# Two layers with experts and an attention block: two more weight slots, and GpSimd's small transfers on the ScalarE and SyncE queues

## The chip, the cores and the metric

The kernel runs on one core of a Trainium2 chip. The metric is the device time of one execution in microseconds. Of the kernel before there are three timed runs, 1488.46, 1492.85 and 1492.9 us, with a median of 1492.85 us, and one profiled execution of its own.

## The reference, cut to what matters

The input is 256 tokens of 1024 float32 values. A first block has two layers, each a mixer with a residual and layer norm, then a mixture of 16 experts with the same. A second block is one layer of attention and a gated feed-forward part with a short convolution.

```python
def ec_moe(x, w_router, w_gate, w_up, w_down):         # 16 experts, 32 tokens each
    aff = softmax(x @ w_router)
    gates, idx = lax.top_k(swapaxes(aff, 1, 2), 32)
    xin = x[bidx, idx]
    h = silu(xin @ w_gate[e]) * (xin @ w_up[e])         # 32x1024 @ 1024x1024, twice
    out = (h @ w_down[e]) * gates
    return zeros_like(x).at[bidx, idx].add(out)

x = layer_norm(ALPHA * x + mlstm_mixer(x), ln_g[0, 0], ln_b[0, 0])
x = layer_norm(ALPHA * x + ec_moe(x, layer 0), ln_g[0, 1], ln_b[0, 1])
x = layer_norm(ALPHA * x + gla_mixer(x), ln_g[1, 0], ln_b[1, 0])
x = layer_norm(ALPHA * x + ec_moe(x, layer 1), ln_g[1, 1], ln_b[1, 1])
h = x + moba_attention(rms_norm(x, attn_norm) @ w_qkv, rel_bias) @ w_o
h = h + conv_ffn(rms_norm(h, ffn_norm), w_up, conv_w, conv_b, w_down)
return rms_norm(h, final_norm)
```

## The kernel before, in words

**Stages.** In the profiled execution the first mixer (mLSTM) runs from 0 to some 140 us, the first layer's experts to 575, the second mixer (GLA) to 720, the second layer's experts to 1160, then the query, key and value products, attention and the output product to 1285, and the feed-forward part to the end.

**Weights.** All weights come as units of 1 MB, a tile of 128 partitions by 2048 float32 values, from the pool `big`, in one fixed order (`stream`). They are loaded by SyncE (SP) alone, at L141 where a unit is flat and at L147 where it is laid out by column blocks. An expert takes twelve units: four of `moe_w_gate`, four of `moe_w_up`, four of `moe_w_down`. A layer's experts therefore take 192 units. We number the units from the first gate unit of layer 0, so that layer 1's experts are units 208 to 399; expert e of a layer has its gate units at 12e to 12e+3, then up, then down.

**Slots.** `SLOTS` is the number of such tiles that may be in use. Working tiles of the mixers (`slab`) come out of the same pool, and `pump` loads on while there is room:

```python
    def pump():
        while stream and mem["wts"] < SLOTS - max(mem["keep"], mem["act"]):
            emit_load()
```

`keep` holds slots back for working tiles that will be wanted soon; it is 1 to 10 in the stages and rises at the end of a layer's experts (8 + 2i from expert 10, 14 + 2i from expert 14, where i is the layer).

**One expert.** TensorE multiplies the 32 picked tokens with the gate and up units (L978), ScalarE (ACT) applies the silu to the gate's product (L993), VectorE multiplies by the up product (L994), TensorE transposes (L998), VectorE copies (L1002), TensorE multiplies with the four down units (L1025), and ACT and VectorE copy the result out (L1037). The last expert of a layer has sums woven in (L987), warm-up products (L186), and its own down product (L1058, L1071). `extra` hangs other work on experts: `gla_prep` (L1170 to L1180) on expert 9 of layer 0, rows for the second mixer (`spread`, L342) on expert 12 of it, the tables of the relative bias (L1222) on experts 6 to 13 of layer 1 and their rows (`bucket_rows`, L1212 and L1213) on expert 5, and `attn_rows` (L342, L1235) on expert 14.

**What sets the order.** A scheduler orders the instructions of each engine when the kernel is built; each engine then runs its own list in order, and a step that waits holds all behind it on that engine. The transfers that SP and ACT issue share eight completion semaphores, DMAHW0 to DMAHW7, given out in turn over both engines. A transfer on one of them carries a wait for the transfer that had the semaphore before it. In the kernel before, where ACT issues only three transfers, all at the start, that means that SP keeps at most eight units on the way. The transfers that GpSimd (POOL) issues have semaphores of their own (DMASW). There are 26 of them: the rows of the layer norms (L342, L943), ten of `gla_prep` (L1170, L1175, and eight at L1180), two of `bucket_rows`, `attn_norm` (L1235), three of the convolution (L1287 to L1289), and the rows of the last norms (L342).

Of the kernel before, what the change touches and what calls it, by code (L numbers as in the profile page):

```python
# [10 lines left out]
F32 = mybir.dt.float32  # L11
# [6 lines left out]
P = 128  # L18
S = 256
# [7 lines left out]
RSQ = 1.5 ** (1 / 7)  # L27
RSQ_BITS = float(round(0x5F3759DF + 0.5 * math.log2(0.5 * RSQ) * (1 << 23)) - (1 << 31))

SLOTS = 25  # L30
NSPLIT = 3
NE0 = 1
E0 = 32 * NE0
# [11 lines left out]
def two_layer_mixer_moe_then_attention_kernel(  # L45
# [9 lines left out]
    nc = tc.nc  # L55

    const = ctx.enter_context(tc.tile_pool(name="const", bufs=1))
    big = ctx.enter_context(tc.tile_pool(name="big", bufs=SLOTS))
    work = ctx.enter_context(tc.tile_pool(name="work", bufs=3))
# [7 lines left out]
    def slab(dt=F32):  # L67
        mem["act"] += 1
        assert mem["act"] + mem["wts"] <= SLOTS, mem
        t = big.tile([P, 2048], dt, tag="slot", name="slab")  # L70
        return t
# [10 lines left out]
    def kcols(w, c0, n):  # L82
        return w[:, c0:c0 + n].rearrange("(k p) f -> p k f", p=P)
# [52 lines left out]
    def emit_load(parts=1):  # L136
        src = stream.pop()
        mem["wts"] += 1
        t = big.tile([P, 2048], F32, tag="slot", name="unit")
        if len(src.shape) == 2:  # L140
            nc.sync.dma_start(t[:, :2048], src)  # L141
            ready.insert(0, t[:, :2048].rearrange("p (k f) -> p k f", k=2))
            return
        v = t[:, :2048].rearrange("p (k f) -> p k f", k=src.shape[1])
        n = src.shape[2] // parts
        for j in range(parts):
            nc.sync.dma_start(v[:, :, j * n:j * n + n], src[:, :, j * n:j * n + n])  # L147
        ready.insert(0, v)
# [5 lines that stand above are left out]
    def take():  # L154
        if not ready:
            assert mem["act"] + mem["wts"] < SLOTS, mem
            emit_load()
# [14 lines left out]
    def aux():  # L172
        b = psp.tile([P, 512], F32, tag="aux", name="aux")
        return b
# [39 lines left out]
    x_tok = tok(xt)  # L214
    for t in range(2):
        nc.sync.dma_start(x_tok[:, t, :], x[0, t * P:(t + 1) * P, :])
    ones = const.tile([P, P], F32, name="ones")
    ones_row = ones[:, 0:1].to_broadcast([P, S])
    ident = const.tile([P, P], F32, name="ident")
    nc.gpsimd.memset(ones, 1.0)  # L220
    nc.gpsimd.affine_select(ident, ones, pattern=[[1, P]], compare_op=OP.is_equal, fill=0.0, base=0,
                            channel_multiplier=-1)
    gpad = slab()
# [41 lines left out]
    def open_split(n=NSPLIT, claim=False):  # L265
        wsp[:0] = [slab(F32R) for _ in range(n)]
        if claim:
            for t in wsp[:n]:
                nc.gpsimd.memset(t[:, 0:1].bitcast(F32), 0.0)
# [66 lines left out]
        tr[:] = [transposed(src, use, bank)]  # L336
        return h, l

    def spread(dst, tmp, *rows):
        n = 1024 * len(rows)  # L340
        for j, row in enumerate(rows):
            nc.gpsimd.dma_start(tmp[0:1, 1024 * j:1024 * j + 1024], row)  # L342
        nc.gpsimd.partition_broadcast(dst[:, :n], tmp[0:1, :n], channels=P)

    def mm3(o, ah, al, bh, bl, first, stop):
# [460 lines left out]
    def moe(i, r, extra, finish):  # L806
# [129 lines left out]
        def residual():  # L936
            for t in range(2):
                nc.gpsimd.tensor_tensor(st["oh"][:, t], st["oh"][:, t], af[:, t, :, None].to_broadcast([P, 16, 32]),
                                        op=OP.mult)
            gbc = slab()  # L940
            for j, row in enumerate((ln_g, ln_b)):
                tmp = st["sg"][0:1].rearrange("p g t -> p (g t)")
                nc.gpsimd.dma_start(tmp, row[i, 0:1])  # L943
                nc.gpsimd.partition_broadcast(gbc[:, 1024 * j:1024 * j + 1024], tmp, channels=P)
            for j, op in enumerate((OP.mult, OP.add)):
                for t in range(2):
                    nc.gpsimd.tensor_tensor(n[:, t, :], n[:, t, :], gbc[:, 1024 * j:1024 * j + 1024], op=op)
# [12 lines left out]
        for e in range(NE):  # L960
# [50 lines left out]
            if e == 3 + 1:  # L1011
                gather(NE0 + 8, 8 - NE0)
                residual()
# [21 lines left out]
            for j in range(4):  # L1035
                eng = nc.vector.tensor_copy if j // 2 else nc.scalar.copy
# [128 lines left out]
    def gla_prep():  # L1165
        t = slab()
        cmask = t[:, 256:296].bitcast(U8).rearrange("p (l c) -> p l c", l=5)
        cmask6 = t[:, 320:352].bitcast(U8)
        sx = t[:, 512:672]
        nc.gpsimd.dma_start(sx, c_xor)  # L1170
        for lev in range(5):
            nc.vector.tensor_scalar(cmask[:, lev, :], sx[:, P:160], float(1 << lev), None, op0=OP.is_ge)
        nc.vector.tensor_scalar(cmask6, sx[:, :P], 64.0, None, op0=OP.is_ge)
        gv = t[:, 0:256].rearrange("p (k c) -> p k c", k=8)
        nc.gpsimd.dma_start(gv, kcols(gla_w_in[0], 3072, 32))  # L1175
        gwp = t[:, 1024:2048]
        nc.gpsimd.memset(gwp, 0.0)
        for j in range(4):
            for d in range(2):
                nc.gpsimd.dma_start(gwp[32 * j + 16 * d:32 * j + 16 * d + 16, 512 * d:512 * d + 512], gla_gate_w[0, d])  # L1180
        prep.extend((gv, gwp, cmask, cmask6))

    close_split(len(wsp))
# [2 lines left out]
    def end_rows():  # L1186
        gb, o = slab(), slab()
        spread(gb, o, ln_g[0, 1:2], ln_b[0, 1:2])
        ends.extend((gb, o))
# [11 lines left out]

    sub[:] = [nc.vector]
    x1, xh, xl = moe(0, r, {9: gla_prep, 12: end_rows}, finish0)
    r = gla(xh, xl, x1, prep)

    buckets = []

    def bucket_rows():
        tmp = slab()
        relT, cb = tmp[:33, 0:16], tmp[:33, 128:512]  # L1210
        nc.vector.memset(relT[32:33, :], 1.0)
        nc.gpsimd.dma_start(relT[:32, :], rel_bias.rearrange("h b -> b h"), allow_slow_non_contiguous=True)  # L1212
        nc.gpsimd.dma_start(cb, c_bucket)  # L1213
        buckets.extend((relT, cb))
        table.extend(slab()[:, :2048].rearrange("p (h c) -> p h c", h=8) for _ in range(2))

# [15 lines left out]
    def attn_rows():  # L1232
        gb, ag, o = slab(), slab(), slab()
        spread(gb, o, ln_g[1, 1:2], ln_b[1, 1:2])
        nc.gpsimd.dma_start(o[0:1, 0:1024], attn_norm)  # L1235
        nc.gpsimd.partition_broadcast(o[:, 1024:2048], o[0:1, 0:1024], channels=P)
        for j in range(2):
            nc.gpsimd.tensor_tensor(ag[:, 1024 * j:1024 * j + 1024], gb[:, 1024 * j:1024 * j + 1024],
                                    o[:, 1024:2048], op=OP.mult)
        ends.extend((gb, ag, o))  # L1240
# [15 lines left out]

    sub[:] = [nc.vector]
    extra = {5: bucket_rows, 14: attn_rows}
    for step in range(8):
        extra[6 + step] = lambda step=step: tables(step)  # L1260
# [10 lines left out]
    def rms_cols(rs, pb, rb):  # L1271
        dg = w1()
        for t in range(2):
            nc.vector.tensor_scalar(dg[:, t * P:(t + 1) * P], ident, rs[t], None, op0=OP.mult)
        for t in range(2):
            nc.tensor.matmul(pb[:, t * P:(t + 1) * P], ones, dg[:, t * P:(t + 1) * P], start=True, stop=True)
        nc.vector.tensor_copy(rb, pb[:, :S])
        return rb
# [5 lines left out]
    ccol = misc[:, 0:176]  # L1284
    cv = misc[:, 768:1024].rearrange("p (a c) -> p a c", a=2)
    cw_rows = conv_w[0].rearrange("k (f c) -> (k f) c", c=P)
    nc.gpsimd.dma_start(cv[:, 0, :], cw_rows[0:128, :])  # L1287
    nc.gpsimd.dma_start(cv[0:4, 1, :], cw_rows[128:132, :])
    nc.gpsimd.dma_start(cv[4:48, 1, :], conv_b.rearrange("o (f c) -> (o f) c", c=P))  # L1289
    rb = rms_cols(rs, aux(), misc[:, 256:512])  # L1290
    rbb = rb[:, None, :].to_broadcast([P, 2, S])
    qk = slab()
# [3 lines left out]
    for a in range(4):  # L1296
# [5 lines left out]
        for hi in range(4):  # L1302
            f, r0 = hi // 2, 64 * (hi % 2)
# [16 lines left out]
        for hi in range(4):  # L1320
# [5 lines left out]
            o = 384 * (len(eT) % 5)  # L1326
# [12 lines left out]
    for c in range(2):  # L1339
# [3 lines left out]
        for a in (2 * c, 2 * c + 1):  # L1343
            po = aux().rearrange("p (t h e) -> p t h e", t=2, h=4)
            for hi in range(4):
                h = 4 * a + hi
# [14 lines left out]
    close_ring("b")  # L1361
    drop(7)
    gfin, frow = slab(), slab()
    spread(gfin, frow, final_norm.rearrange("(o d) -> o d", o=1), ffn_norm)
    open_split(2)
    h1 = token_out(uh, ul, h0, 1.0, 6)
    close_split(2)
# [75 lines left out]
    for t in range(2):  # L1443
# [10 lines left out]
        for c in range(2):  # L1454
            o = h2[:, t, c * 512:(c + 1) * 512]
# [55 lines left out]
```

## Time and profile before

| what | value |
|---|---|
| median of three runs | 1492.85 us (1488.46 to 1492.9) |
| profiled execution, its own time | 1491.23 us |
| span of its trace | 1489.5 us |
| TensorE busy | 1288.0 us, 86% of the span |
| VectorE, ScalarE, GpSimd busy | 552.3, 376.3 and 105.0 us |
| moved by transfers | 492.41 MB, 331 GB/s in the mean |
| of that on SP's queue | 489.93 MB |
| of that on GpSimd's queue | 864 packets, 0.66 MB |

The busy shares are means over stages with different limits. In the two stages of experts the transfer engines are busy all the time; in the mixers, in attention and in the feed-forward part TensorE is. What the change is worth has to be read stage by stage. The span is 1.7 us shorter than the execution's own time; sums are made against the latter.

### The profile page before, as it was taken

What the parts mean: (1) busy time and instruction counts of PE and PEld (TensorE: products, weight loads), DVE (VectorE), ACT (ScalarE), POOL (GpSimd) and SP (SyncE); (2) the same over time, 40 slices, a digit from 0 to 9 for tenths busy, and PEclk for the clock granted to TensorE, in tenths of its full rate; (3) what the DMA queues carried; (4) which work ended last, traced back from release to release, by engine and by line L of the source; (5) the groups of instructions that cost most, each with busy time, mean ns of one, the idle gap of its engine ahead of it and who ended that gap; (6) DMA issues with size and microseconds to landing.
All of it is one profiled execution on the core that took longest, in us unless ns stands there. A gap on an engine that the chain in (4) does not pass through costs nothing.

```text
span 1489.5 us, 27080 instructions
## 1 busy us (share of the span) xinstructions
PE 1288.0 (86%) x11749; PEld 906.5 (61%) x11749; DVE 552.3 (37%) x1130; ACT 376.3 (25%) x605; POOL 105.0 (7%) x84
## 2 busy tenths in 40 slices
PE   9999976776656678999996669999998999999998
PEld 8887633222222225988653327556664798899997
DVE  5784201111001005876410100200101875697776
ACT  5562100000000002754310000000000464365554
POOL 1000002100100000100000210000002400010000
PEclk9999988687678689999997866876769999999999
DMA  9957999999999999847899999999999943645400
GB/s 286 372 228 308 408 421 420 421 421 420 398 421 420 420 420 353 296 171 287 342 420 421 416 419 420 421 420 421 420 420 383 363 167 114 225 149 192 170 1 29
DMA packets 129302, 492.41 MB, mean 331 GB/s; under 512 B 11570, under 2 KB 68037, under 8 KB 81056
## 3 DMA queue, kind: packets, MB, share of 16 engines
q1 hardware_dynamic: 127216, 489.93, 83.6%
q8 instruction: 92, 1.51, 0.4%
q0 software_dynamic: 864, 0.66, 0.2%
q10 hardware_dynamic: 1104, 0.10, 0.1%
q14 instruction: 26, 0.21, 0.0%
HBM read 489.61 MB, written 1.05 MB: 329 GB/s over the span
## 4 chain that ended last, share of the span: by engine, by line
PE 52%; DMA 42%; DVE 4%; POOL 1%; issue 1%; ACT 1%; DVEq 0%; SPq 0%; ACTq 0%; POOLq 0%
DMA unit<-in_moe_w_down_dram 16%; DMA unit<-in_moe_w_up_dram 13%; DMA unit<-in_moe_w_gate_dram 12%; PE acc L347 8%; PE acc L346 8%; PE acc L348 8%; PE acc L978 6%; PE aux L1222 4%; PE aux L1025 3%; PE aux L346 1%; PE aux L347 1%; PE aux L348 1%; PE aux L933 1%; PE aux L630 1%; PE aux L1043 1%
## 5 line engine op out<-in xcount | busy, mean ns | idle before, releaser
L978 PE MATMUL acc<-unit,slab 128*32 128x256 f32 x3840 | 316.4, 471 | 114.0 <-DMA unit<-in_moe_w_up_dram 60.0
L978 PEld LDWEIGHTS acc<-unit,slab 128*32 128x32 f32 x3840 | 129.8, 129 | 293.5 <-DMA unit<-in_moe_w_up_dram 90.9
L347 PE MATMUL acc<-slab 128*128 128x256 f32 (+1 forms) x896 | 276.7, 309 | 0.6 <-DVE slab L298 0.4
L346 PE MATMUL acc<-slab 128*128 128x256 f32 (+1 forms) x896 | 273.4, 310 | 2.8 <-ACT slab L326 2.8
L348 PE MATMUL acc<-slab 128*128 128x256 f32 (+1 forms) x896 | 273.9, 309 | 0.0
L298 DVE TENSOR_TENSOR slab<-unit,slab 128x1024 fp32r<-128x1024 f32 x156 | 198.7, 1279 | 81.0 <-ACT slab L297 79.1
L297 ACT ACTIVATE slab<-unit 128x1024 fp32r<-128x1024 f32 x152 | 160.2, 1058 | 154.1 <-PE acc L347 75.7
L1025 PE MATMUL aux<-unit,w 128*32 128x256 f32 x1920 | 152.6, 453 | 40.0 <-DMA unit<-in_moe_w_down_dram 28.8
L346 PEld LDWEIGHTS acc<-slab 128*128 128x128 f32 x896 | 170.8, 191 | 12.8 <-ACT slab L326 3.6
L347 PEld LDWEIGHTS acc<-slab 128*128 128x128 f32 x896 | 170.9, 191 | 11.0 <-issue 1.7
L348 PEld LDWEIGHTS acc<-slab 128*128 128x128 f32 x896 | 170.9, 191 | 8.7 <-issue 1.1
L994 DVE TENSOR_TENSOR w<-w,acc 128x256 f32<-128x256 f32 x32 | 13.5, 421 | 368.6 <-PE acc L978 356.0
L1037 ACT COPY slab<-aux 32x256 f32<-32x256 f32 x60 | 21.7, 361 | 421.2 <-PE aux L1025 420.3
L1025 PEld LDWEIGHTS aux<-unit,w 128*32 128x32 f32 x1920 | 63.3, 125 | 106.2 <-DMA unit<-in_moe_w_down_dram 48.3
L1037 DVE COPY slab<-aux 32x256 f32<-32x256 f32 x60 | 25.4, 424 | 221.2 <-ACT slab L1037 216.2
L1222 PEld LDWEIGHTS aux<-slab 33*128 33x128 f32 x512 | 91.7, 276 | 14.2 <-issue 14.2
L1222 PE MATMUL aux<-slab 33*128 33x16 f32 x512 | 94.0, 331 | 0.0
L993 ACT ACTIVATE w<-acc 128x256 f32<-128x256 f32 x32 | 12.3, 383 | 279.2 <-PE acc L978 279.2
L933 PEld LDWEIGHTS aux<-slab 128*128 128x128 f32 x192 | 30.8, 206 | 8.7 <-issue 7.8
L933 PE MATMUL aux<-slab 128*128 128x128 f32 (+1 forms) x192 | 35.7, 329 | 0.0
L347 PE MATMUL aux<-slab 128*128 128x512 f32 x88 | 34.3, 390 | 0.0
L348 PE MATMUL aux<-slab 128*128 128x512 f32 x88 | 34.2, 389 | 0.0
(346 smaller groups left out, 1212.9 us busy)
## 6 DMA issues: line engine op xcount, KB each, us to landing
unit<-in_moe_w_gate_dram SPq DMA_DIRECT2D x128, 1024.0 KB, 19.8
unit<-in_moe_w_up_dram SPq DMA_DIRECT2D x128, 1024.0 KB, 19.8
unit<-in_moe_w_down_dram SPq DMA_DIRECT2D x128, 1024.0 KB, 19.8
unit<-in_w_up_dram SPq DMA_DIRECT2D x22, 1024.0 KB, 5.8
unit<-in_gla_w_in_dram SPq DMA_DIRECT2D x12, 1024.0 KB, 12.4
unit<-in_w_qkv_dram SPq DMA_DIRECT2D x12, 1024.0 KB, 12.2
unit<-in_mlstm_w_in_dram SPq DMA_DIRECT2D x11, 1024.0 KB, 13.7
unit<-in_w_down_dram SPq DMA_DIRECT2D x11, 1024.0 KB, 5.0
```

What stands on the lines that cost most here:

```text
L297: nc.scalar.activation(h, src, AF.Copy)
L298: eng.tensor_tensor(l, src, h.bitcast(F32), op=OP.subtract)
L346: nc.tensor.matmul(o, ah, bh, start=first, stop=False)
L347: nc.tensor.matmul(o, ah, bl, start=False, stop=False)
L348: last[:] = [nc.tensor.matmul(o, al, bh, start=False, stop=stop)]
L630: mm = nc.tensor.matmul(o, E[d][:, h, o0:o0 + P], v[s][:, h, :], start=i == 0, stop=i == len(terms) - 1)
L933: nc.tensor.matmul(o, n_cols(t, k), ohf[:, t], start=t == 0, stop=t == 1)
L978: mm = nc.tensor.matmul(pb[32 * j:32 * j + 32, :256], picked(kk, e), unit[:, k, 256 * j:256 * j + 256], start=kk == 0, stop=kk == 7)
L1025: mm = nc.tensor.matmul(py[32 * j:32 * j + 32, :256], hT[:, kk % 2, 32 * (kk // 2):32 * (kk // 2) + 32], unit[:, k, 256 * j:256 * j + 256] ...
L1037: eng(yb[32 * eg:32 * eg + 32, g % 2, 256 * j:256 * j + 256], py[32 * j:32 * j + 32, :256])
L1043: nc.tensor.matmul(pb, st["sg"][:, g, t * P:(t + 1) * P], yb[:, g % 2, cs], start=True, stop=True)
L1222: nc.tensor.matmul(pb[:, 16 * j:16 * j + 16], cb[:, 256 - c:384 - c], relT, start=True, stop=True)
```

## The change

`SLOTS` goes from 25 to 27. The reserve that the program sets aside for GpSimd's transfer descriptors is set to 512 B (`dynamic_dma_scratch_size`), and the constant tile of ones shrinks from 128 columns to one that is read as a broadcast. GpSimd then issues no transfers: those of the norm rows, of `gla_prep`, of `bucket_rows` and of `attn_rows` go to ACT's queue, those of the convolution and of the last norms' rows to SP's. Line numbers of the changed kernel are one higher from L218 on.

```diff
-SLOTS = 25
+SLOTS = 27
...
-    ones = const.tile([P, P], F32, name="ones")
-    ones_row = ones[:, 0:1].to_broadcast([P, S])
+    one = const.tile([P, 1], F32, name="one")
+    ones = one.to_broadcast([P, P])
+    ones_row = one.to_broadcast([P, S])
...
-    nc.gpsimd.memset(ones, 1.0)
+    nc.gpsimd.memset(one, 1.0)
...
-    def spread(dst, tmp, *rows):
+    def spread(dst, tmp, *rows, eng=None):
         n = 1024 * len(rows)
         for j, row in enumerate(rows):
-            nc.gpsimd.dma_start(tmp[0:1, 1024 * j:1024 * j + 1024], row)
+            (eng or nc.scalar).dma_start(tmp[0:1, 1024 * j:1024 * j + 1024], row)
...
-                nc.gpsimd.dma_start(tmp, row[i, 0:1])
+                nc.scalar.dma_start(tmp, row[i, 0:1])
...
-        nc.gpsimd.dma_start(sx, c_xor)
+        nc.scalar.dma_start(sx, c_xor)
...
-        nc.gpsimd.dma_start(gv, kcols(gla_w_in[0], 3072, 32))
+        nc.scalar.dma_start(gv, kcols(gla_w_in[0], 3072, 32))
...
-                nc.gpsimd.dma_start(gwp[32 * j + 16 * d:32 * j + 16 * d + 16, 512 * d:512 * d + 512], gla_gate_w[0, d])
+                nc.scalar.dma_start(gwp[32 * j + 16 * d:32 * j + 16 * d + 16, 512 * d:512 * d + 512], gla_gate_w[0, d])
...
-        nc.gpsimd.dma_start(relT[:32, :], rel_bias.rearrange("h b -> b h"), allow_slow_non_contiguous=True)
-        nc.gpsimd.dma_start(cb, c_bucket)
+        nc.scalar.dma_start(relT[:32, :], rel_bias.rearrange("h b -> b h"), allow_slow_non_contiguous=True)
+        nc.scalar.dma_start(cb, c_bucket)
...
-        nc.gpsimd.dma_start(o[0:1, 0:1024], attn_norm)
+        nc.scalar.dma_start(o[0:1, 0:1024], attn_norm)
...
-    nc.gpsimd.dma_start(cv[:, 0, :], cw_rows[0:128, :])
-    nc.gpsimd.dma_start(cv[0:4, 1, :], cw_rows[128:132, :])
-    nc.gpsimd.dma_start(cv[4:48, 1, :], conv_b.rearrange("o (f c) -> (o f) c", c=P))
+    nc.sync.dma_start(cv[:, 0, :], cw_rows[0:128, :])
+    nc.sync.dma_start(cv[0:4, 1, :], cw_rows[128:132, :])
+    nc.sync.dma_start(cv[4:48, 1, :], conv_b.rearrange("o (f c) -> (o f) c", c=P))
...
-    spread(gfin, frow, final_norm.rearrange("(o d) -> o d", o=1), ffn_norm)
+    spread(gfin, frow, final_norm.rearrange("(o d) -> o d", o=1), ffn_norm, eng=nc.sync)
...
-    nc = _bacc.Bacc("TRN2", target_bir_lowering=False, num_devices=1)
+    nc = _bacc.Bacc("TRN2", target_bir_lowering=False, num_devices=1, dynamic_dma_scratch_size=512)
```

The lists of TensorE and VectorE stay nearly as they were. Three places of the other lists matter here.

ACT near the end of layer 1's experts, before: the silus are those of experts 13 and 14, with the copies of experts 12, 13 and 14 between them. In brackets stand the semaphores that a row waits on.

```order
L1037 COPY slab<-aux 32x256 [waits PE_49,Activation_49]
L1037 COPY slab<-aux 32x256 [waits Activation_49]
L993 ACTIVATE w_7521<-acc 128x256 [waits DVE_49,PE_49]
L1037 COPY slab<-aux 32x256 [waits PE_49,Activation_49]
L1037 COPY slab<-aux 32x256 [waits Activation_49]
L993 ACTIVATE w_7679<-acc 128x256 [waits DVE_49,PE_49]
```

The same place of the changed kernel, from the silu of expert 13 to that of expert 14:

```order
L994 ACTIVATE w_7525<-acc 128x256 [waits DVE_49,PE_49]
L1038 COPY slab<-aux 32x256 [waits PE_49,Activation_49]
L1038 COPY slab<-aux 32x256 [waits Activation_49]
L343 DMA slab<-in_ln_g_dram 1x1024 [waits DMAHW3_49,DMAHW2_49,DMAHW4_49,DMAHW1_49,DMAHW7_49,DMAHW0_49,PE_49]
L343 DMA slab<-in_ln_b_dram 1x1024 [waits DMAHW5_49]
L994 ACTIVATE w_7683<-acc 128x256 [waits DVE_49,PE_49]
```

Two transfers now stand ahead of expert 14's silu. The DMAHW4 that the first waits for was last given to unit 391, the last gate unit of expert 15, and the DMAHW5 of the second to unit 392, expert 15's first up unit.

ACT around expert 9 of layer 0 in the changed kernel; before, these rows were the same without the three DMA rows:

```order
L994 ACTIVATE w_2839<-acc 128x256
L1171 DMA slab<-in_c_xor_dram 128x160
L1176 DMA slab<-in_gla_w_in_dram 128x8x32
L1181 DMA slab<-in_gla_gate_w_dram 16x512 x8
L1038 COPY slab<-aux 32x256 x2
L994 ACTIVATE w_2992<-acc 128x256
```

Ten transfers stand behind the silu of expert 9 and ahead of that of expert 10. By the semaphores they carry, the first waits for unit 131 and the last for unit 138. In the same way two transfers of `bucket_rows` now stand ahead of the silu of expert 6 of layer 1, behind units 291 and 292, and two of `spread` ahead of that of expert 13 of layer 0, behind units 167 and 168.

On SP, the three transfers of the convolution now stand between the first and the second unit of `w_o`:

```order
L147 DMA unit<-in_w_o_dram 128x2x1024 [waits DMAHW4_49,PE_49]
L1288 DMA slab<-in_conv_w_dram 128x128 [waits DVE_49,DMAHW5_49,PE_49,Activation_49]
L1289 DMA slab<-in_conv_w_dram 4x128 [waits DMAHW6_49]
L1290 DMA slab<-in_conv_b_dram 44x128 [waits DMAHW7_49]
L147 DMA unit<-in_w_o_dram 128x2x1024 [waits DMAHW0_49,DVE_49,Activation_49]
```

In the kernel before the four `w_o` rows followed each other.

## Rows read from the trace of the kernel before

**Rows 1.** The page's chain that ended last, shares of the span by engine

```profile
PE 52%; DMA 42%; DVE 4%; POOL 1%; issue 1%; ACT 1%; DVEq 0%; SPq 0%; ACTq 0%; POOLq 0%
```

**Rows 2.** Stretches: length, busy us by engine, TensorE clock, DMA share, GB/s

```profile
131.00:145.00 14.00, 12.24 (x86) 9.64 (x86) 7.00 (x29) 4.63 (x10) 0.00 (x0) 1.00 0.55 231
160.00:575.00 415.00, 290.52 (x3123) 125.82 (x3123) 41.41 (x96) 21.47 (x55) 24.25 (x23) 0.79 1.01 416
713.00:727.00 14.00, 12.28 (x86) 9.70 (x87) 6.87 (x29) 4.50 (x10) 0.00 (x0) 1.00 0.67 278
760.00:1160.00 400.00, 346.90 (x3526) 213.00 (x3524) 48.23 (x116) 19.40 (x49) 26.25 (x18) 0.77 1.01 415
900.00:1100.00 200.00, 192.08 (x1728) 129.22 (x1729) 24.55 (x52) 6.63 (x18) 0.00 (x0) 0.73 1.01 420
1160.00:1490.00 330.00, 318.85 (x2194) 290.56 (x2192) 238.87 (x422) 177.62 (x280) 38.50 (x20) 0.99 0.45 153
```

**Rows 3.** SP's waits, 760 to 1126: total us, times, longest

```profile
SPq L141 <- DMA unit<-in_moe_w_down_dram: 102.2, 48, 3.5
```

**Rows 4.** SP's waits, 120 to 150, same columns

```profile
SPq L141 <- PE acc L978: 16.9, 3, 13.5
```

**Rows 5.** SP's timeline before and in layer 0's experts: start, duration, transfers

```profile
127.00 4.36 SPq L141 DMA_DIRECT2D unit<-in_moe_w_down_dram  x4
144.97 4.88 SPq L141 DMA_DIRECT2D unit<-in_moe_w_gate_dram  x4
...
192.58 7.78 SPq L141 DMA_DIRECT2D unit<-in_moe_w_gate_dram  x4
202.51 7.76 SPq L141 DMA_DIRECT2D unit<-in_moe_w_up_dram  x4
```

**Rows 6.** ACT's timeline, silus and copies; in brackets idle time and its releaser

```profile
372.47 0.38 ACT L993 ACTIVATE w<-acc 128x256 f32<-128x256 f32 x1 [9.71 <-PE acc L978]
...
435.61 0.38 ACT L993 ACTIVATE w<-acc 128x256 f32<-128x256 f32 x1 [8.75 <-PE acc L978]
...
832.81 0.38 ACT L993 ACTIVATE w<-acc 128x256 f32<-128x256 f32 x1 [6.57 <-PE acc L978]
...
1105.63 0.75 ACT L1037 COPY slab<-aux 32x256 f32<-32x256 f32 x2 [16.24 <-PE aux L1025]
1118.90 0.38 ACT L993 ACTIVATE w<-acc 128x256 f32<-128x256 f32 x1 [12.52 <-PE acc L978]
```

**Rows 7.** TensorE's timeline in layer 1's experts, same columns

```profile
885.20 1.94 PE L978 MATMUL acc<-unit,slab 128*32 128x256 f32 x16 [0.54 <-DMA unit<-in_moe_w_gate_dram]
...
1112.80 9.48 PE L978 MATMUL acc<-unit,slab 128*32 128x256 f32 x128
...
1123.92 3.66 PE L1025 MATMUL aux<-unit,w 128*32 128x256 f32 x64 [0.52 <-DVE w L1002]
...
1134.19 1.07 PE L978 MATMUL acc<-unit,slab 128*32 128x256 f32 x16 [0.37 <-DMA unit<-in_moe_w_gate_dram]
...
1136.77 1.07 PE L978 MATMUL acc<-unit,slab 128*32 128x256 f32 x16 [0.45 <-DMA unit<-in_moe_w_up_dram]
...
1150.11 1.10 PE L1058 MATMUL aux<-unit,w 128*32 128x64 f32 x64 [0.75 <-DMA unit<-in_moe_w_down_dram]
...
1153.12 1.10 PE L1058 MATMUL aux<-unit,w 128*32 128x64 f32 x64 [0.85 <-DMA unit<-in_moe_w_down_dram]
...
1157.58 2.22 PE L1071 MATMUL aux<-slab 128*128 128x256 f32 x8
```

**Rows 8.** The page's transfers by kind: issuer, count, KB each, us to landing

```profile
unit<-in_moe_w_gate_dram SPq DMA_DIRECT2D x128, 1024.0 KB, 19.8
...
slab<-in_gla_gate_w_dram POOLq DMA_DIRECT2D x8, 32.0 KB, 7.7
```

**Rows 9.** ACT's queue at the start of the program, an issue of a transfer

```profile
2.02 0.46 ACTq L226 DMA_DIRECT2D slab<-in_mlstm_w_in_dram  x1
```

## Prediction

> **What bounds the kernel now.** I read the chain that ended last first: it is on TensorE for 52% of the span and on transfers for 42% [rows 1], so no single engine bounds the kernel and the stages have to be taken apart. In the two stages of experts, 160 to 575 and 760 to 1160, the transfer engines are busy throughout (share 1.01, 415 and 416 GB/s) while TensorE is busy for 290.5 of 415 and 346.9 of 400 us [rows 2]. SP waits there for transfers and for hardly anything else: 102.2 us in 48 waits on down units alone [rows 3], and two more rows of that view, for gate and up units, read alike. A unit lands every 2.48 us: four gate units are issued at 192.58 and the next four at 202.51, 9.93 us later [rows 5]; it is 19.8 us on its way [rows 8], so that eight are. From 1160 on TensorE is busy for 318.9 of 330 us and transfers have a share of 0.45 [rows 2]; what comes earlier or later at 1160 comes earlier or later at the end.
>
> Two further facts matter. Ahead of each stage of experts SP stands still because no slot is free: it issues down units until 131.4 and the next gate unit only at 144.97 [rows 5], and the longest single wait there is 13.5 us on TensorE [rows 4]; the transfer share falls to 0.55 in 131 to 145 and to 0.67 in 713 to 727 [rows 2]. And in the middle of layer 1's experts transfers are not alone on the edge: between 900 and 1100, with the bias tables, TensorE is busy for 192 of 200 us at a granted clock of 0.73 [rows 2].
>
> **The slots.** Two more slots let SP issue two more units in each of the two gaps. Transfers that run without pause from there to the stage's end then run two units, 2 x 2.48 = 4.97 us, ahead. There is room for it: the idle part of the transfer engines is 0.45 x 14 = 6.3 us in the first gap and 0.33 x 14 = 4.6 us in the second [rows 2], so the second lead may be 4.6 instead of 4.97. The first lead passes through the second mixer, where TensorE sets the pace, and adds to the second: units of layer 1 land 9.6 to 9.9 us earlier. I take **-9.9 us** for the landing of unit 392.
>
> **The moved transfers, on ACT.** A transfer on ACT or SP waits for the eighth transfer before it, and on ACT it now holds the silus. Before, the rows on GpSimd held nobody. The listing shows what each waits for; the costs are the distance to the next thing that wants ACT.
>
> Layer 0, expert 9: ten transfers stand behind the silu at 372.47 and the last waits for unit 138. The silu of expert 11 followed its gate unit 135 at 435.61 [rows 6], so unit 138 lands three units, 7.4 us, later, near 443, and near 438 with the lead. The silu of expert 10 cannot run before; TensorE stops after that expert's up units, 127 being the last, eleven units before 138, and so for 11 x 2.48 = 27 us. Expert 12's pair waits for units 167 and 168, five after the last that TensorE can use: 12.4 us more. Together this is 39.7 us of work put off. Transfers go on meanwhile: a unit waits for the freeing of a slot 22 units back, and eleven are on hand. From 438 to the stage's end near 570 there are 132 us, of which TensorE needed 290.5/415 = 70% [rows 2], so some 39.6 us can be caught up. I take **0** for the end of layer 0's experts, with 0 and 11 as bounds (rival C).
>
> Layer 1, expert 5: two transfers behind the silu at 832.81 wait for units 291 and 292. Unit 292 is taken at 885.20 [rows 7], and at 875.3 with the lead. The silu of expert 6 comes then. Eight units are on hand, at up to 1.94 us each [rows 7] 15.5 us: TensorE is back at about 891 with what it did at 892 before, ahead of the tables. I take **0**.
>
> Layer 1, expert 13: two transfers stand behind the copies at 1105.63 and ahead of the silu of 1118.90 [rows 6]; they wait for 391 and 392. Unit 392 is taken at 1136.77 [rows 7], with the lead 1126.8, eight us after the silu ran before. Here nothing is left to catch up with. From there: an issue 0.46 [rows 9], the silu 0.38 [rows 6], from the end of the up units at 1122.28 to the down product at 1123.92 1.64, and from there to the end of the last sum, 1159.80, 35.88 us in which TensorE waited 3.2 for transfers (0.37, 0.45, and three of 0.75 to 0.85 of which the first two are shown) [rows 7], so 32.7. That is 35.2 us behind unit 392; before it was 1159.80 - 1136.77 = 23.03. The hold costs **+12.1 us**. It also lets TensorE idle for some ten us, and the row at 1112.80 shows what an engine coming off a lower clock pays: eight units in 9.48 us, against 2 x 3.66 at the full clock [rows 7]: **+2.2**.
>
> What waits behind it is GpSimd's work on those rows. At up to 7.7 us a small transfer [rows 8] they have landed by 1135, some 25 us before the norm that wants them. The transfer after expert 15's silu waits for units long landed. I take 0 for both.
>
> The Trainium skill (DMA: Bandwidth & Descriptors, "Anatomy of one DMA — SWDGE (gpsimd) path") states that the transfer engines wait for no semaphore, and that any such wait happens on the sequencer that issues. Nothing in the trace of before shows ACT held by one, since ACT issues only at the start; by this rule the hold on the silu is as I take it.
>
> **The rest.** On SP the convolution's three transfers wait for the end of layer 1's experts and stand ahead of three units of `w_o`, which are wanted tens of us later; from 1160 on transfers have half their time free [rows 2]. I take 0, bounds 0 and +2.5 (one unit). GpSimd loses 26 issues, and is nowhere on the path (1% of the chain [rows 1]). The bytes of the small transfers stay. The broadcast of ones feeds the same products; its price is 0 with a bound of a few tenths on either side.
>
> **The sum.** -9.9 + 12.1 + 2.2 = +4.4 on the profiled execution's 1491.23: 1495.6, say **1496 us**. The median of the runs is 1.6 above that execution, so that on it the sum would be 1497.2; differences under 0.3% (4.5 us) can't be told from no change.
>
> **Rivals.**
> A is this forecast. Its own range is 1492 to 1500: the second lead of 4.6 or less, the clock's term from 0 to 6.
>
> B: the waits on ACT hold nothing that matters, because the silus come first or the transfers ahead have landed. Then the lead is all there is: 1491.2 - 9.9 = 1481.3, faster. For it: ACT is idle 12.5 us ahead of the very silu [rows 6]. Against it: that idle time lies ahead of the transfers' place, and the semaphores are written in the listing. The Trainium skill (DMA: Bandwidth & Descriptors, "Issuing engines are not separate DMA queues") says that issuing from several engines only saves the time of issuing; by that rule alone moving the transfers changes nothing, and B's time follows. The rows of before can't refute it for ACT.
>
> C: the ten transfers of expert 9 and the pair of expert 12 cost more than layer 0 gives back. A unit at 1.94 us [rows 7] in a step of 2.48 leaves 22% instead of 30%: 29 of 39.7 us are caught up by the end, 10.7 are not, 1495.6 + 10.7 = 1506.3, slower. It decides from the point where TensorE, back from its stop, needs more than 70% of the transfers' time. For it: units right after a wait take 1.94 us. Against it: TensorE without waits came to 0.92 a unit at 1123.92 [rows 7].
>
> D: after the last hold the clock stays where it was in the tables, 0.73 [rows 2]: 35.2/0.73 is 13.0 more instead of 2.2, which gives 1506.
>
> E: the slots aren't filled and there is no lead: 1491.2 + 12.1 + 2.2 = 1505.5. Against it: in the listing each unit waits for the freeing of one two further back.
>
> **Chances.** A 0.52, B 0.20, C 0.15, D 0.08, E 0.05. Of A about 0.3 lie within 0.3% of before and 0.22 above. Faster by over 0.3%: B and a little of A, 0.21. Within: 0.33, with C half caught up. Slower: 0.46. Since both signs have weight the range spans B to C, 1480 to 1506; what is outside is the upper part of C and D.
>
> **What would show it.** The transfer share in 131 to 145 should rise to about 0.9, and units 391 and 392 should be taken ten us earlier. ACT's queue should show waits of about 70 us behind expert 9's silu in layer 0, 50 behind expert 5's and some 20 behind the copies of expert 13 in layer 1, each followed by a stop of TensorE at the transposition (27, 13 and about ten us). The last sum of layer 1's experts should end near 1164. I am wrong if TensorE's stop in layer 1 is short, if the sum ends before 1155, or if layer 0's experts end later than before.

## Result and the profile after

The changed kernel takes 1500.13 us (median of four runs, 1499.39 to 1503.42) against 1492.88 us for the kernel before beside it: a ratio of 1.0061 with an interval of 1.0046 to 1.0076, slower by 0.6% (the two medians alone are 7.2 us, 0.5%, apart). The prediction was 1496 us, in a range of 1480 to 1506, with slower as the likeliest sign. The profiled run is the slowest of the four, 1503.42 us; the median is the better measure of its size.

The page's chain by engine, beside [rows 1]: nine points have gone from transfers, eight of them to TensorE.

```profile
PE 60%; DMA 33%; DVE 4%; issue 1%; POOL 1%; ACT 1%; ACTq 0%; DVEq 0%; SPq 0%; POOLq 0%
```

Stretches of the changed kernel with the columns of [rows 2]. The first four answer to rows there; the others show the start, the stop of TensorE in layer 0 and the end of layer 1's experts.

```profile
131.00:145.00 14.00, 12.17 (x92) 9.49 (x89) 7.19 (x31) 5.22 (x10) 0.00 (x0) 1.00 0.59 249
160.00:575.00 415.00, 267.23 (x3239) 128.89 (x3240) 44.30 (x106) 21.30 (x55) 17.28 (x10) 0.77 1.01 412
713.00:727.00 14.00, 12.21 (x86) 9.63 (x86) 6.94 (x29) 4.57 (x10) 0.00 (x0) 1.00 0.66 276
760.00:1160.00 400.00, 315.63 (x3271) 198.81 (x3267) 42.42 (x94) 21.14 (x50) 17.58 (x10) 0.76 1.02 414
...
60.00:80.00 20.00, 20.00 (x116) 17.99 (x115) 13.67 (x39) 7.76 (x11) 0.00 (x0) 1.00 0.99 403
...
405.00:442.00 37.00, 2.64 (x18) 0.91 (x18) 1.56 (x4) 1.11 (x3) 0.00 (x0) 0.50 0.90 352
...
1104.00:1135.00 31.00, 10.50 (x136) 5.24 (x139) 1.60 (x4) 0.38 (x1) 0.00 (x0) 0.61 1.01 418
1135.00:1160.00 25.00, 24.87 (x245) 12.21 (x245) 1.70 (x4) 4.17 (x6) 3.60 (x2) 0.91 1.04 335
```

The same stretches of the kernel before, where they were not shown:

```profile
60.00:80.00 20.00, 20.00 (x118) 17.98 (x116) 13.65 (x41) 8.18 (x11) 0.00 (x0) 1.00 0.75 308
...
405.00:442.00 37.00, 21.72 (x230) 7.91 (x226) 2.35 (x10) 1.49 (x4) 0.00 (x0) 0.78 1.01 420
```

ScalarE now waits for transfers. Its waits by line (us in total, times, longest), of the changed kernel:

```profile
ACT slab L1038 <- DMA unit<-in_moe_w_gate_dram: 72.5, 2, 45.4
ACT slab L1038 <- DMA slab<-in_gla_gate_w_dram: 71.8, 1, 71.8
...
ACT slab L892 <- DMA unit<-in_moe_w_down_dram: 60.7, 2, 30.9
...
ACT w L994 <- DMA unit<-in_moe_w_up_dram: 32.9, 1, 32.9
```

The last of these is the one that counts. ScalarE's timeline near the end of layer 1's experts, beside the last two rows of [rows 6]:

```profile
1130.05 0.23 ACTq L343 DMA_DIRECT2D slab<-in_ln_g_dram  x1
1132.39 0.23 ACTq L343 DMA_DIRECT2D slab<-in_ln_b_dram  x1
1132.72 0.38 ACT L994 ACTIVATE w<-acc 128x256 f32<-128x256 f32 x1 [32.89 <-DMA unit<-in_moe_w_up_dram]
```

TensorE's timeline there, beside [rows 7]:

```profile
1104.16 9.47 PE L979 MATMUL acc<-unit,slab 128*32 128x256 f32 x128
1133.61 0.70 PE L999 MATMUL aux<-ident,w 128*128 128x128 f32 x2 [19.99 <-DVE w L995]
1134.83 6.04 PE L1026 MATMUL aux<-unit,w 128*32 128x256 f32 x64 [0.52 <-DVE w L1003]
...
1168.65 0.65 PE L1059 MATMUL aux<-unit,w 128*32 128x64 f32 x32 [1.79 <-issue]
1169.23 2.24 PE L1072 MATMUL aux<-slab 128*128 128x256 f32 x8
```

The silu of expert 14 could have run by 1113.6, when the expert's products end, and runs at 1132.72, 0.33 us behind the issue of the transfer that waits for unit 392. TensorE stands for 20 us. The last sum ends at 1171.47, before at 1159.80: 11.7 us, and the two profiled executions are 12.2 apart (1503.42 and 1491.23). So all but half a microsecond of the loss is in place by the end of layer 1's experts.

### The profile page after: what moved, and what is told of

Read it like the earlier page. It is cut to its first block, busy times and chain, and to the rows that moved or that the text cites. A ratio compares the mean times of both kernels' runs of the same rounds, so it can differ in the third digit from the quotient of the medians.

```text
span 1501.7 us, 27042 instructions
## 1 busy us (share of the span) xinstructions
PE 1241.9 (83%) x11749; PEld 902.4 (60%) x11749; DVE 552.4 (37%) x1130; ACT 376.2 (25%) x605; POOL 89.7 (6%) x58
## 4 chain that ended last, share of the span: by engine, by line
PE 60%; DMA 33%; DVE 4%; issue 1%; POOL 1%; ACT 1%; ACTq 0%; DVEq 0%; SPq 0%; POOLq 0%
DMA unit<-in_moe_w_down_dram 11%; DMA unit<-in_moe_w_up_dram 11%; DMA unit<-in_moe_w_gate_dram 10%; PE acc L979 9%; PE acc L348 8%; PE acc L347 8%; PE acc L349 8%; PE aux L1223 5%; PE aux L1026 4%; PE aux L934 2%; PE aux L348 1%; PE aux L347 1%; PE aux L349 1%; DMA slab<-in_gla_w_in_dram 1%; PE aux L1044 1%
## 5 line engine op out<-in xcount | busy, mean ns | idle before, releaser
L979 PE MATMUL acc<-unit,slab 128*32 128x256 f32 x3840 | 276.7, 432 | 55.1 <-DMA unit<-in_moe_w_up_dram 28.6
L979 PEld LDWEIGHTS acc<-unit,slab 128*32 128x32 f32 x3840 | 126.1, 121 | 199.1 <-issue 49.7
L1026 PE MATMUL aux<-unit,w 128*32 128x256 f32 x1920 | 146.8, 446 | 22.2 <-DMA unit<-in_moe_w_down_dram 12.0
L999 PE MATMUL aux<-ident,w 128*128 128x128 f32 x64 | 17.9, 368 | 96.0 <-DVE w L995 96.0
L1223 PEld LDWEIGHTS aux<-slab 33*128 33x128 f32 x512 | 85.4, 259 | 12.7 <-issue 12.7
L1223 PE MATMUL aux<-slab 33*128 33x16 f32 x512 | 87.8, 317 | 0.0
L934 PE MATMUL aux<-slab 128*128 128x128 f32 (+1 forms) x192 | 39.8, 353 | 55.9 <-ACT slab L892 55.9
L999 PEld LDWEIGHTS aux<-ident,w 128*128 128x128 f32 x64 | 10.0, 203 | 113.1 <-DVE w L995 111.3
```

The source lines that it names most:

```text
L934: nc.tensor.matmul(o, n_cols(t, k), ohf[:, t], start=t == 0, stop=t == 1)
L979: mm = nc.tensor.matmul(pb[32 * j:32 * j + 32, :256], picked(kk, e), unit[:, k, 256 * j:256 * j + 256], start=kk == 0, stop=kk == 7)
L999: mm = nc.tensor.transpose(pT[:, j * P:(j + 1) * P], src, ident)
L1026: mm = nc.tensor.matmul(py[32 * j:32 * j + 32, :256], hT[:, kk % 2, 32 * (kk // 2):32 * (kk // 2) + 32], unit[:, k, 256 * j:256 * j + 256] ...
L1223: nc.tensor.matmul(pb[:, 16 * j:16 * j + 16], cb[:, 256 - c:384 - c], relT, start=True, stop=True)
```

## Experiments

A ratio is to the kernel before, timed beside each run. The fence shows the edit or its core; what each theory expected stands as it was written beforehand. The pair is the two transfers (`ln_g` and `ln_b`) that `attn_rows` puts ahead of expert 14's silu; the hold is the wait of that silu behind them; the lead is how much earlier a unit is issued than in the kernel before.

**The moves without the slots.**

```diff
-SLOTS = 27
+SLOTS = 25
```

> The changed kernel with 25 slots: only the moves of the small transfers are left. Theory H (the moved transfers hold ACT's silus, the two extra slots give a lead of some 4 us that the end of layer 1's experts sees): the lead goes and the holds stay, so about 1504, 4 us above the changed kernel, and the last sum of layer 1's experts ends near 1176. Rival S (the moves cost nothing; the slots, or what was done to find room for them, cost the 7 us): as before, 1493.

1505.74 us, ratio 1.0092 [1.0074, 1.0109]. The moves alone cost 13.7 us of 1492.5; the two slots take 4.6 of it back (1.0092 to 1.0061). In its trace the units at the end of layer 1's experts are issued 5.9 us behind the kernel before, and expert 14's silu runs at 1137.82.

**The slots without the moves.** All small transfers go back to GpSimd; two of them are cut into four and two pieces.

```diff
-            (eng or nc.scalar).dma_start(tmp[0:1, 1024 * j:1024 * j + 1024], row)
+            (eng or nc.gpsimd).dma_start(tmp[0:1, 1024 * j:1024 * j + 1024], row)
...
-        nc.scalar.dma_start(gv, kcols(gla_w_in[0], 3072, 32))
+        src = kcols(gla_w_in[0], 3072, 32)
+        for k in range(0, 8, 2):
+            nc.gpsimd.dma_start(gv[:, k:k + 2, :], src[:, k:k + 2, :])
```

> 27 slots, the reserve of 512 B and the one column of ones as in the changed kernel, but all transfers issued by GpSimd as before (two of them cut into pieces, since the small reserve holds too few descriptors for them whole: the load of gla_w_in into four, rel_bias into two). Theory H: no silu is held, and the lead of 4 to 10 us is all that is left, 1483 to 1489. Rival S: as slow as the changed kernel, 1500. A third outcome, 1493, would say that a lead never reaches the end.

1483.41 us, ratio 0.9941 [0.9926, 0.9956]: faster than both kernels. It keeps 27 slots, the reserve of 512 B and the one column. So what cost the time is where the transfers were moved, and nothing else in the change.

**The transfers of attn_rows alone.** In the changed kernel only these three go back to GpSimd:

```diff
-        spread(gb, o, ln_g[1, 1:2], ln_b[1, 1:2])
-        nc.scalar.dma_start(o[0:1, 0:1024], attn_norm)
+        spread(gb, o, ln_g[1, 1:2], ln_b[1, 1:2], eng=nc.gpsimd)
+        nc.gpsimd.dma_start(o[0:1, 0:1024], attn_norm)
```

> The changed kernel with the three transfers of attn_rows (expert 14 of layer 1) back on GpSimd; all other moves and the 27 slots stay. Theory H with the hold on expert 14's silu as the one that costs (16 us in the trace): the end of layer 1's experts is set by the last down unit again, 4.3 us earlier than before, so about 1489. Rival: the earlier holds (experts 4 and 5 of layer 1, 4, 9 and 12 of layer 0) cost as much and leave TensorE late at the end: 1495 to 1500.

1486.78 us, ratio 0.9963 [0.995, 0.9975]. Three transfers of 4 KB carry 14.6 us (0.9963 to 1.0061).

**The ten transfers of gla_prep alone**, back on GpSimd in the changed kernel (that of `gla_w_in` in four pieces):

```diff
-        nc.scalar.dma_start(sx, c_xor)
+        nc.gpsimd.dma_start(sx, c_xor)
```

> The changed kernel with the transfers of gla_prep (expert 9 of layer 0; gla_w_in cut into four pieces) back on GpSimd; all else stays. In the trace of the changed kernel the lead falls from 5.0 to 2.4 us at these transfers and to nothing by the start of layer 1's experts. If the ten transfers on ACT alone did that, layer 1's units come 2.4 to 5 us earlier and the time is 1495 to 1498. If the first lead is lost at the end of layer 0's experts whatever came ahead, 1500 as the changed kernel.

1498.62 us, ratio 1.0043 [1.0029, 1.0058]: 2.7 us less than the changed kernel, about what the uncertainty of such a difference is (some 3 us), and between the two expected outcomes. The trace decides: the last units of layer 1's experts have a lead of 8.5 us (4.3 in the changed kernel), so the ten transfers did cost some of it. The pair waits for the same units 391 and 392, and the silu runs at 1128.53 instead of 1132.72: this lead does reach the held silu, and the profiled execution takes 1499.52 us instead of 1503.42.

**The reverse: of the kernel before, only the transfers of attn_rows moved to ScalarE**, with 25 slots:

```diff
-        spread(gb, o, ln_g[1, 1:2], ln_b[1, 1:2])
-        nc.gpsimd.dma_start(o[0:1, 0:1024], attn_norm)
+        spread(gb, o, ln_g[1, 1:2], ln_b[1, 1:2], eng=nc.scalar)
+        nc.scalar.dma_start(o[0:1, 0:1024], attn_norm)
```

> The kernel before, 25 slots and all else as it was, with only the three transfers of attn_rows (expert 14 of layer 1) issued by ACT. This is the hold of expert 14's silu by itself, without a lead. The prediction's terms (12.1 for the hold and 2.2 for the clock) give 1492 + 14.3 = 1506; the trace of the changed kernel, 39.1 us from the landing of unit 392 to the last sum against 23.0 before, gives 16, so 1508. Rival (the end only came late there because earlier holds had put TensorE back): under 1497.

1502.78 us, ratio 1.0073 [1.0058, 1.0088]: +10.5 us in the medians (1492.3 beside it), 10.9 by the ratio. That is far from the rival's under 1497, but 3 to 5 us below both figures expected. Its ScalarE timeline (line numbers of the kernel before) tells why, and why it is less than the 14.6 at 27 slots:

```profile
1128.60 0.47 ACTq L342 DMA_DIRECT2D slab<-in_ln_g_dram  x1
1131.05 0.23 ACTq L342 DMA_DIRECT2D slab<-in_ln_b_dram  x1
1131.38 0.38 ACT L993 ACTIVATE w<-acc 128x256 f32<-128x256 f32 x1 [25.41 <-DMA unit<-in_moe_w_gate_dram]
```

With 25 slots the pair waits for units 389 and 390, both gate units, with 27 for 391 and 392: SP stands two units further ahead when ScalarE draws its semaphores. The expected figures were reckoned with unit 392; unit 390 lands two units, 5 us, before it. So with more slots the units come earlier and the pair waits for later ones, and part of what the slots give is taken away again as long as this hold is there. From e1_moves25 to the changed kernel the last units of layer 1's experts come 10.1 us earlier, the silu only 5.1 (1137.82 to 1132.72), and the time falls by 4.6 us; without the moves the slots give 8.8 (e2_gp27).

**The same with 27 slots from the other side: e2_gp27 with the ten of gla_prep on ScalarE.**

```diff
-        nc.gpsimd.dma_start(sx, c_xor)
+        nc.scalar.dma_start(sx, c_xor)
```

> The 27 slots with all transfers on GpSimd (1483.4 in the first runs), and of them only the ten of gla_prep issued by ACT. Theory: the hold of some 70 us behind expert 9's silu is caught up by TensorE before layer 0's experts end, and what stays is the 2.5 us by which the stream of weights stands still, so 1486. Rival C of the prediction (TensorE not level by the end of the layer): 1490 or more. No cost at all: 1483.

1486.05 us, ratio 0.996 [0.9945, 0.9975]. 2.8 us above e2_gp27; the time above 1490 that rival C asked for isn't there. Its trace shows how they cost anything at all. In 405 to 442, where TensorE stands, transfers have a share of 0.90 here too, as in the changed kernel, and 1.02 in e2_gp27. The first fence is e6_prep_act27, the second e2_gp27:

```profile
405.00:442.00 37.00, 2.82 (x26) 1.12 (x22) 1.69 (x4) 1.11 (x3) 0.00 (x0) 0.50 0.90 354
```

```profile
405.00:442.00 37.00, 21.70 (x214) 7.62 (x210) 2.51 (x11) 1.10 (x3) 0.00 (x0) 0.69 1.02 405
```

**ScalarE's transfers on SP instead.**

```diff
-            (eng or nc.scalar).dma_start(tmp[0:1, 1024 * j:1024 * j + 1024], row)
+            (eng or nc.sync).dma_start(tmp[0:1, 1024 * j:1024 * j + 1024], row)
```

> The changed kernel with all its ACT transfers on SP instead. If what costs is that the waiting engine holds silus, and not the queue or the shared semaphores, SP holds only further loads and most of the lead is left: 1483 to 1489. If small transfers among the weights' semaphores thin out the stream, more than 1490.

1493.5 us, ratio 1.0018 [1.0008, 1.0028]: 4.5 us above the 1483 to 1489 of the first theory, and in the range of its rival, over 1490. No silu is held, but the transfers now stand in the stream of units: at unit 396 the lead is 2.3 us, in e2_gp27 7.3. SP's timeline at the end of layer 1's experts:

```profile
1124.43 17.50 SPq L147 DMA_DIRECT2D unit<-in_moe_w_down_dram  x3
1142.03 0.39 SPq L343 DMA_DIRECT2D slab<-in_ln_g_dram  x1
1142.46 0.24 SPq L343 DMA_DIRECT2D slab<-in_ln_b_dram  x1
1149.35 0.22 SPq L1236 DMA_DIRECT2D slab<-in_attn_norm_dram  x1
1149.67 0.39 SPq L147 DMA_DIRECT2D unit<-in_moe_w_down_dram  x1
```

The last down unit stands behind three rows and is issued at 1149.67, in the kernel before at 1144.34; its sum waits for it and the rows themselves come late for the norm. TensorE pays for both:

```profile
1155.20 1.10 PE L1059 MATMUL aux<-unit,w 128*32 128x64 f32 x64 [2.90 <-DMA unit<-in_moe_w_down_dram]
...
1166.31 2.07 PE L1116 MATMUL acc<-w,slab 128*128 128x128 f32 x8 [4.39 <-DVE slab L1103]
```

**The reserve and the column alone**, e2_gp27 with 25 slots:

```diff
-SLOTS = 27
+SLOTS = 25
```

> The kernel with all transfers on GpSimd, the reserve of 512 B, the cut transfers and the one column of ones, at 25 slots. If the two slots are all that makes 27 faster, this is the kernel before, 1492. If the smaller reserve or the column of ones does something by itself, it shows as a difference from 1492.

1491.88 us, ratio 0.9999 [0.999, 1.0009]. They do nothing that shows; the gain of e2_gp27 is that of the slots.

**The order turned round.** The changed kernel with the pair still on ScalarE's queue, but behind expert 14's silu instead of ahead of it:

```diff
-            nc.scalar.activation(hs, pgu[0][:, :S], AF.Silu)
+            silu[:] = [nc.scalar.activation(hs, pgu[0][:, :S], AF.Silu)]
...
-        spread(gb, o, ln_g[1, 1:2], ln_b[1, 1:2])
+        with tc.issue_after(silu[0].ins):
+            spread(gb, o, ln_g[1, 1:2], ln_b[1, 1:2])
```

> The changed kernel with one order turned round: the three transfers of attn_rows stay on ACT's queue, but the pair now stands behind expert 14's silu instead of ahead of it. If what costs is that the silu of expert 14 stands behind a transfer that waits for units 391 and 392, then the silu comes when its gate product is done, near 1114, TensorE's stop of 20 us at the transposition goes, and only copies and the silu of expert 15 can be held, which want those units anyway. The last sum of layer 1's experts ends near 1155 and the median falls to that of e3_tail_gp, 1486 to 1489. If it is instead the mere presence of these transfers on ACT, or the units that ACT's semaphores hold back, the last sum stays at 1166 or later and the median at 1495 to 1500. The gap put down to 'issue' between the last sums should be 0.3 us or less if it goes with the hold, and 1.8 if it goes with the transfers.

1486.81 us, ratio 0.9961 [0.9948, 0.9975], as with the transfers on GpSimd (1486.78). ScalarE's timeline (two line numbers on from the kernel before):

```profile
1105.34 0.38 ACT L995 ACTIVATE w<-acc 128x256 f32<-128x256 f32 x1 [10.43 <-PE acc L980]
1128.15 0.23 ACTq L344 DMA_DIRECT2D slab<-in_ln_g_dram  x1
1130.49 0.23 ACTq L344 DMA_DIRECT2D slab<-in_ln_b_dram  x1
1130.81 0.75 ACT L1039 COPY slab<-aux 32x256 f32<-32x256 f32 x2 [25.09 <-PE aux L989]
```

The transfers wait for the same units 391 and 392, which land 1.9 us earlier in this trace, and now hold the copies behind them, from 1119.9, where the product that they copy ends, to 1130.81; nobody waits for those. This is the run that settles the mechanism: one silu that stands behind a waiting transfer costs some 14 us, not the transfers, their semaphores or the queue.

**One slot instead of two**, e2_gp27 with 26:

```diff
-SLOTS = 27
+SLOTS = 26
```

> The kernel e2_gp27 (512 B of reserve, one column of ones, all small transfers on GpSimd) with 26 slots, between e8_gp25 (25 slots, 1491.9) and e2_gp27 (27 slots, 1483.4). If each slot lets one more unit start in the two gaps ahead of the experts, the gain is shared about evenly: the unit at the end of layer 1's experts is issued 4 us ahead of before (e8_gp25: 1.2, e2_gp27: 7.3), and the median lies at 1487 to 1488.5. If a gap gives room for one unit alone, or if two slots are needed before one more whole unit fits, it lies within 1 us of 1483.4 or of 1491.9.

1487.72 us, ratio 0.9974 [0.9958, 0.9989]: with 25, 26 and 27 slots 0.9999, 0.9974 and 0.9941. The first slot gives 3.7 us, the second 4.9, each uncertain by some 3. In its trace the unit at the end of layer 1 leads by 5.3 us, more than expected, but part of that is lost at the last sums (below).

## Why the prediction was right, and where it was off

The account, from the ratios above, each step times 1492.5 us (a difference of two ratios is uncertain by some 3 us):

| step | from the kernels | measured | predicted |
|---|---|---|---|
| two slots | before to e2_gp27 | -8.8 | -9.9 |
| ten transfers of gla_prep on ScalarE | e2_gp27 to e6_prep_act27 | +2.8 | 0 (0 to 11) |
| other rows on ScalarE and SP | e6_prep_act27 to e3_tail_gp | +0.4 | 0 (0 to 2.5) |
| pair ahead of expert 14's silu | e3_tail_gp to after | +14.6 | +12.1 and +2.2 |
| sum | | +9.1 | +4.4 |

The order of the steps matters, since the slots give less beside the hold (e1_moves25), and the second and third step are within the uncertainty. All that is off, less lead and a slightly dearer hold, lies on the slow side; nothing cancelled, and the median came 4 us above the forecast.

**The hold** was right in its place, its units and, nearly, its size. From the issue behind unit 392's landing (1132.39) to the end of the last sum it is 39.1 us, predicted 35.2 + 2.2 = 37.4; the rest is about the 1.79 us of "issue" in TensorE's row at 1168.65. The sum was forecast to end near 1164 and ends at 1171.47: 5.5 us of that are lead that isn't there, 1.7 are the hold. TensorE stands for 20 us where some ten were forecast, because it is done with expert 14's up units at 1113.6, before at 1122.3. That adds nothing to the price, which runs from the landing of unit 392. The clock's term was right as well: the down product takes 6.04 us, 2.4 more than in [rows 7], at the border of two stretches with a granted clock of 0.61 (1104 to 1135) and 0.91 (1135 to 1160). Rival D wanted it to stay at 0.73 and falls.

**The lead** was right in size at first and wrong in its place. Leads are taken here from the times at which SP issues a unit in the two traces. Unit 48, issued at 192.58 before [rows 5], comes at 187.68, 4.90 us earlier, two units as predicted:

```profile
187.68 7.79 SPq L141 DMA_DIRECT2D unit<-in_moe_w_gate_dram  x4
```

But the transfer share of 131 to 145 rose from 0.55 to 0.59 and not to 0.9: the slots were filled as soon as the pool had room, at 60 to 80 us, where the share rose from 0.75 to 0.99 (95 GB/s more over 20 us, 1.9 MB). In 131 to 145 SP waits for the same product of TensorE as before, two units further on. The step that failed is the room: I took it from the idle stretch that ends at the experts, and it has to be taken from all the idle time since the slots were last all in use. In the second mixer the same reading gave 4.6 to 5.0, and 3.0 us were gained (a lead of 1.23 us at unit 236 and of 4.36 at unit 252; in e2_gp27 4.66 and 7.65).

**The ten transfers** were costed at their worst for TensorE, and that part held: it stops for 33.8 us (27 predicted) and catches up, and layer 0's last sum ends at 581.6, before at 583.3. The first row is the changed kernel, the second the kernel before:

```profile
577.86 3.78 PE L1072 MATMUL aux<-slab 128*128 128x256 f32 x8
```

```profile
581.11 2.23 PE L1071 MATMUL aux<-slab 128*128 128x256 f32 x8
```

What the step left out are the transfers. ScalarE's and SP's timelines of the changed kernel:

```profile
416.68 0.36 ACTq L1171 DMA_DIRECT2D slab<-in_c_xor_dram  x1
419.12 0.40 ACTq L1176 DMA_DIRECT2D slab<-in_gla_w_in_dram  x1
421.73 16.99 ACTq L1181 DMA_DIRECT2D slab<-in_gla_gate_w_dram  x8
438.82 0.75 ACT L1038 COPY slab<-aux 32x256 f32<-32x256 f32 x2 [71.83 <-DMA slab<-in_gla_gate_w_dram]
```

```profile
397.75 7.80 SPq L141 DMA_DIRECT2D unit<-in_moe_w_gate_dram  x4
409.22 20.63 SPq L141 DMA_DIRECT2D unit<-in_moe_w_up_dram  x4
438.30 1.93 SPq L141 DMA_DIRECT2D unit<-in_moe_w_down_dram  x4
```

Ten small transfers take ten turns of the eight semaphores over 22 us, 2.4 us apart in the mean. SP, whose next units come behind them in the turn, needs 20.63 us for four up units where 7.62 were enough before. Fewer units are on the way, the share falls to 0.90, and the lead goes from 4.98 us at unit 124 to 2.56 at unit 152. "Transfers go on meanwhile" was the sentence that was wrong: they went on at nine tenths. Rival C had the place but not the reason, and its 10.7 us did not come.

**Layer 1's early holds** cost nothing that shows, as forecast for expert 5 (ScalarE is free at 880.6, predicted 875.3, after a wait of 27 us and not 50; TensorE's stop is 15 us, predicted 13). One I had not seen at all: a row of `ln_b` (L944) now stands among expert 4's instructions and stops TensorE for longer than any other in that layer.

```profile
842.40 3.35 PE L934 MATMUL aux<-slab 128*128 128x224 f32 x8 [29.04 <-ACT slab L892]
```

It too is caught up: the changed kernel issues unit 300 0.26 us behind before and unit 364 again 4.22 us ahead. TensorE catches up with every hold that comes early; of the 20 us that it stands behind the last one it gets back no more than it would have waited for units anyway, and 14.6 are paid.

**The rivals.** B, nothing held, falls by the 32.89 us of ScalarE's row, and e9_behind shows what it would have been: 1486.8, not 1481.3. By the rule of the Trainium skill that B leaned on (DMA: Bandwidth & Descriptors, "Issuing engines are not separate DMA queues") the move would only save issue time; here the issuing engine's order decided the sign. E falls by the lead.

In the profiled run alone unit 392 comes 4.4 us earlier (1136.77 in [rows 7], 1132.39) and the hold costs 16.1 (39.1 against 23.0), which gives the 11.7 seen there. Up to expert 13 of layer 1 the changed kernel, e3_tail_gp and e9_behind issue the same units in the same order, and their leads behind it (unit 376) are 4.3, 5.5 and 6.2 us: a single trace moves by 2 us. That is why the account goes by the timed runs.

## What to carry to other kernels

Before a small transfer is put on the queue of an engine that computes, read in the order which transfer it waits for and which instruction stands behind it: its price is at most the distance from that instruction's own time to the landing of that other transfer. Where enough work is left to catch up with, it is forgiven; where none is, it is paid, less what the work behind would have waited anyway (14.6 of 20 us here). A stream that comes earlier helps such an instruction in full only if the transfer still waits for the same member of it (e4_prep_gp); two more slots made it wait for a later one, and half of the gain was gone (e1_moves25 to the changed kernel). If it must be there, put it behind the last instruction that somebody waits for (1486.8 instead of 1500.1 us), or leave it on an engine that nobody waits for (1483.4).

## What was not expected of the hardware

TensorE's gap marked "issue" in the sums at the end of layer 1's experts is 1.79 us in the changed kernel, 1.88 in e5_tail_act25 and 1.45 in e10_gp26, but 0.18 in e2_gp27, always within the last 64 products of L1059 (L1058):

```profile
1151.27 0.64 PE L1059 MATMUL aux<-unit,w 128*32 128x64 f32 x28
1153.36 0.75 PE L1059 MATMUL aux<-unit,w 128*32 128x64 f32 x36 [1.45 <-issue]
```

```profile
1148.69 0.64 PE L1059 MATMUL aux<-unit,w 128*32 128x64 f32 x28 [0.79 <-DMA unit<-in_moe_w_down_dram]
1149.51 0.75 PE L1059 MATMUL aux<-unit,w 128*32 128x64 f32 x36 [0.18 <-issue]
```

The first fence is e10_gp26, the second e2_gp27. e10_gp26 holds no silu, so the gap doesn't come from the hold by itself, as had been thought possible. The traces show what falls due there. A transfer of 16 KB of the page's kind "instruction" starts 2.4 to 2.6 us before TensorE goes on: at 1166.24 in the changed kernel (on again at 1168.65), at 1150.87 in e10_gp26 (1153.36), at 1146.99 in e2_gp27 (1149.51). It is the same for each of the 19 TensorE gaps marked "issue" of over 0.6 us in the twelve traces, all of them in the last sums of a layer, with 0.64 to 3.10 us. The row of that kind is the same in all twelve pages (transfers, MB, share of the transfer engines):

```profile
q8 instruction: 92, 1.51, 0.4%
```

So at the end of layer 1 the products seem to wait for their own instructions, and where they wait for a down unit meanwhile, as in e2_gp27, most of that is hidden. At the end of layer 0 a gap of 3.10 us stands in the kernel before and one of 2.58 in the changed one. That the transfer is the cause was not tried by a run.
